# Row-tiled logits and indexer scores in layer 0 of a two-layer attention trunk (one Trainium2 core)

## Chip, cores and metric

One core of one Trainium2 chip runs the whole kernel in one launch. The metric is device time in microseconds, measured around the execution; lower is better. The engines named below: TensorE (PE in the profile, its weight loads PEld), VectorE (DVE), ScalarE (ACT), GpSimd (POOL) and SyncE (SP), which issues the DMAs.

## What is computed

The input x is 256 tokens by 1024 features, float32. Layer 0 is sparse attention with an indexer, layer 1 stick-breaking attention; each is gated, projected and added to the scaled input under a LayerNorm. What matters here is layer 0:

```python
q, k, v, g, qi, wi, ki = jnp.split(x @ w_in, cuts, axis=-1)   # 16 heads of 64; indexer: 8 heads of 64, one ki
q, k, qi, ki = (apply_rope(t) for t in (q, k, qi, ki))
rel = relu(einsum('bqhd,bsd->bqhs', qi, ki) * 64 ** -0.5)
score = einsum('bqhs,bqh->bqs', rel, wi)                      # keys in the same or an earlier chunk of 64
idx = top 64 keys of score, for each query
logits = einsum('bqhd,bqkhd->bhqk', q, k[idx]) * 64 ** -0.5
p = softmax(logits)
y = (einsum('bhqk,bqkhd->bqhd', p, v[idx]) * silu(g)) @ w_out
x = layer_norm(ALPHA * x + y)
```

## The kernel before

Matmul operands are kept in two float32r parts, a high part and the rest (names ending in h and l); a product is three matmuls (high x high, high x low, low x high). Weights come in 80 chunks of 512 KB. `fetch` (L73) issues a chunk's DMA on SyncE into one of four `raw` buffers, ScalarE copies its high part (`wh`, L63) and VectorE subtracts the rest (`wl`, L64); chunks are split two ahead of their use. A projection accumulates in a PSUM bank of the pool `pp` (three banks); transposes, scores, logits and values use the pool `at` (five banks).

Layer 0 begins with the indexer's projection (L208). Rope (`rope`, L191 to L198) is four VectorE steps, two products out of PSUM (L195 `ra`, L196 `rb`) and two sums (L197, L198). ki and qi are transposed to features by tokens and split. The split of ki is `pad_split` (L235): ki stands in both 64-row halves of the transposed tile, and each half is copied to its own 256 columns of a zeroed tile `zpad[0]`, by one ScalarE step (L229) and one VectorE step (L230) a half. With the other rows zero, one matmul over all 128 rows with 2n columns gives the scores of two heads, side by side in one bank.

`select` (L260) is a generator. For each token tile t (n = 128 or 256 keys) it has four steps, each with three such matmuls (`mm3`, L129 to L132), one relu on ScalarE (L270) and two additions on VectorE (L273), and then finds the 64 largest in eight rounds of a VectorE maximum (L279) and a replacement (L280), two rounds a step. `mix` (L119) steps it in turn with the first query, key and value blocks: 4 steps for each of the three blocks, 16 for `select`.

The main loop (L498) then runs eight head pairs through stages, one letter of "kfvFlft" each: k is `keys0` (two transposes of rotated keys, then `pad_split` into `zpad[j % 2]`), l is `logits0` one step later, t is `turn0` (transposes of the weights) two steps later, v is `values0` (`weighted_v`, L341, each head in its 64 columns of the array) three steps later; f takes a piece of the remaining projections, and F does so in the first four steps only. So in steps 4 to 8 the logits directly follow the values. `logits0` (L377) has three matmuls for each token tile through `mm3`; for each tile and head VectorE adds the mask and takes the extreme (L393), ScalarE takes the exponential (L398), VectorE scales (L400, L403).

The order of instructions on each engine's queue is laid down before the run by the framework: it goes by the program's order, and where an instruction isn't ready in its own estimate of times it puts later ones ahead. At run time every queue is worked off in that order. Layer 1 uses `zpad` again, for its queries.

Of the kernel before, what the change touches and what calls it, by code (L numbers as in the profile page):

```python
# [9 lines left out]
F32 = mybir.dt.float32  # L10
F32R = mybir.dt.float32r
AF = mybir.ActivationFunctionType
OP = mybir.AluOpType
# [29 lines left out]
def trunk(ctx: ExitStack, tc: tile.TileContext, x_rows, x_idx, w_all, consts, lnp, out):  # L43
# [13 lines left out]
    def as32(t):  # L57
        return t.bitcast(F32)
# [7 lines left out]
    # activations, feature-major: [feature in tile, tile, token], split in two float32r parts  # L66
# [29 lines left out]
    def load_block():  # L96
        """A quarter of [1024, 512] of a weight matrix after the other: two K tiles a chunk."""
        for _ in range(4):
            yield [w.rearrange("p (k n) -> p k n", k=2) for w in load_chunk()]

    def tok_part(outs, src, wc, c):
        """Adds a chunk's part to the token tiles in outs (tile, PSUM): the activations are stationary."""
# [7 lines left out]
    def tok_block(src):  # L110
        """Yields after every chunk but the last; returns the PSUM tiles."""
# [7 lines left out]
    def mix(*gens):  # L119
        """One step of every generator in turn."""  # L120
# [8 lines left out]
    def mm3(ps, sh, sl, mh, ml, first, last):  # L129
        nc.tensor.matmul(ps, sh, mh, start=first, stop=False)  # L130
        nc.tensor.matmul(ps, sh, ml, start=False, stop=False)
        nc.tensor.matmul(ps, sl, mh, start=False, stop=last)  # L132

    def proj_feat(ps, src, chunk):
        """[128 features, 256 tokens]: the weights are stationary."""
# [6 lines left out]
    # the tensor engine's clock comes up while the first loads are under way  # L142
# [6 lines left out]
    # ---------------------------------------------------------------- loads  # L149
# [33 lines left out]
    zpad = []  # L183
    for i in range(2):
        zh = cst.tile([P, 2, S], F32R, name=f"zh{i}")
        zl = cst.tile([P, 2, S], F32R, name=f"zl{i}")
        nc.gpsimd.memset(as32(zh), 0.0)
        nc.gpsimd.memset(as32(zl), 0.0)
        zpad.append((zh, zl))
# [10 lines left out]
    # ---------------------------------------------------------------- layer 0: indexer  # L200
# [39 lines left out]
    # indexer: qi of two heads stationary, ki moving, once for either head  # L240
    kz = zpad[0]
# [4 lines left out]
    pad_split(kz, pt[:, :S])  # L246
# [12 lines left out]

    def select():  # L260
        for t in range(NT):
            n = (t + 1) * P
            ts = slice(t * P, (t + 1) * P)
            sc = sb.tile([P, n], F32, name=f"sc{t}")
            prev = adm[t]
            for j in range(4):
# [415 lines left out]
```

## Time and profile before

| | us |
|---|---|
| three runs | 319.74, 318.9, 317.7 |
| median | 318.9 |
| span of the profiled execution, first to last instruction | 318.4 |
| what lies around the span (median less span) | 0.5 |
| TensorE busy | 304.0 |
| VectorE busy | 238.5 |
| ScalarE busy | 186.7 |

The profile is of one execution; its own time isn't listed apart from its span. Times in the views are from the span's start. A row of a timeline gives start, length, engine, line, operation, output and inputs, shapes, count, and in brackets the idle time before it and what ended it; consecutive instructions of one kind are one row, and a matmul's length reaches past the start of the next one, so its cost is read from start to start.

### The profile page before, as it was taken

How to read it: one execution, taken by the hardware profiler on the slowest of the kernel's cores; microseconds unless marked ns; L12 is line 12 of the kernel's file. 1: busy time of each engine (PE TensorE's matmuls, PEld its weight loads, DVE VectorE, ACT ScalarE, POOL GpSimd, SP SyncE). 2: the span in 40 equal slices, each digit the busy share in tenths (PEclk: the TensorE clock that was granted, in tenths of full speed). 3: DMA queues.
4: the chain of work that ended last, by engine and by line, in shares of the span. 5: the costliest groups of instructions: out<-in, count | busy, mean ns of one | idle time of the engine just before them, and what ended most of it. 6: DMA issues, size and time to landing. Idle time of an engine off the chain costs nothing.

```text
span 318.4 us, 5179 instructions
## 1 busy us (share of the span) xinstructions
PE 304.0 (95%) x1914; PEld 264.2 (83%) x1914; DVE 238.5 (75%) x514; ACT 186.7 (59%) x365; POOL 7.8 (2%) x16
## 2 busy tenths in 40 slices
PE   8997899996999999999999999999999999999990
PEld 5985788885887899987788889999999999987790
DVE  3777999997998899897389667655677767662475
ACT  5655545664336997876306276556698888965200
POOL 3010000000000000000010100000000000000011
PEclk9999999999899999999999999999999999999997
DMA  7799744784233745665422949866543433000003
GB/s 263 249 324 307 271 141 143 236 264 153 59 95 118 258 136 153 193 203 178 134 66 80 294 134 320 282 192 165 189 148 118 110 103 118 2 1 1 2 2 130
DMA packets 14425, 50.44 MB, mean 158 GB/s; under 512 B 1600, under 2 KB 1728, under 8 KB 14400
## 3 DMA queue, kind: packets, MB, share of 16 engines
q1 hardware_dynamic: 14256, 49.97, 48.9%
q8 instruction: 15, 0.25, 0.4%
q10 hardware_dynamic: 144, 0.14, 0.1%
q14 instruction: 10, 0.08, 0.1%
HBM read 49.05 MB, written 1.05 MB: 157 GB/s over the span
## 4 chain that ended last, share of the span: by engine, by line
PE 73%; DMA 11%; DVE 10%; ACT 3%; issue 2%; DVEq 0%; SPq 0%; ACTq 0%
PE bank L139 29%; PE bank L107 28%; DMA raw<-w_all 9%; DVE wl L64 4%; PE bank L347 3%; DMA raw<-x_idx 2%; ACT wh L63 2%; PE bank L348 1%; PE bank L571 1%; PE bank L130 1%; DVE sc L280 1%; PE bank L549 1%; PE bank L548 1%; PE bank L550 1%; PE bank L132 1%
## 5 line engine op out<-in xcount | busy, mean ns | idle before, releaser
L63 ACT ACTIVATE wh<-raw 128x1024 fp32r<-128x1024 f32 (+2 forms) x89 | 90.1, 1015 | 58.9 <-DMA raw<-w_all 25.7
L64 DVE TENSOR_TENSOR wl<-raw,wh 128x1024 fp32r<-128x1024 f32 (+2 forms) x89 | 103.5, 1164 | 28.1 <-ACT wh L63 27.2
L107 PE MATMUL bank<-wh,xTh 128*128 128x512 f32 x96 | 28.6, 411 | 2.6 <-DVE rb L196 2.5
L107 PE MATMUL bank<-wh,xTl 128*128 128x512 f32 x96 | 27.9, 400 | 0.0
L107 PE MATMUL bank<-wl,xTh 128*128 128x512 f32 x96 | 27.5, 395 | 0.0
L139 PE MATMUL bank<-yTh,wh 128*128 128x256 f32 x192 | 27.4, 285 | 0.0
L139 PE MATMUL bank<-yTl,wh 128*128 128x256 f32 x192 | 26.9, 283 | 0.0
L139 PE MATMUL bank<-yTh,wl 128*128 128x256 f32 x192 | 26.9, 283 | 0.0
L139 PEld LDWEIGHTS bank<-yTh,wh 128*128 128x128 f32 x192 | 24.7, 190 | 1.2 <-DVE sl L64 0.7
L139 PEld LDWEIGHTS bank<-yTh,wl 128*128 128x128 f32 x192 | 24.8, 192 | 0.0
L139 PEld LDWEIGHTS bank<-yTl,wh 128*128 128x128 f32 x192 | 24.7, 192 | 0.0
L107 PEld LDWEIGHTS bank<-wh,xTh 128*128 128x128 f32 x96 | 17.8, 194 | 7.3 <-issue 3.6
L107 PEld LDWEIGHTS bank<-wh,xTl 128*128 128x128 f32 x96 | 18.5, 194 | 3.9
L107 PEld LDWEIGHTS bank<-wl,xTh 128*128 128x128 f32 x96 | 18.0, 188 | 3.7
L107 PE MATMUL bank<-wh,oh 128*128 128x512 f32 (+1 forms) x80 | 20.8, 355 | 0.0
L107 PE MATMUL bank<-wh,ol 128*128 128x512 f32 (+1 forms) x80 | 20.5, 352 | 0.0
L107 PE MATMUL bank<-wl,oh 128*128 128x512 f32 (+1 forms) x80 | 20.4, 350 | 0.0
L557 DVE SCALAR_TENSOR_TENSOR ab<-bank,ab 128x512 f32<-128x512 f32 (+1 forms) x16 | 8.2, 553 | 12.8 <-ACT ab L556 12.8
L107 PEld LDWEIGHTS bank<-wl,oh 128*128 128x128 f32 x80 | 14.0, 188 | 2.2
L107 PEld LDWEIGHTS bank<-wh,ol 128*128 128x128 f32 x80 | 13.9, 188 | 2.3 <-issue 0.2
L107 PEld LDWEIGHTS bank<-wh,oh 128*128 128x128 f32 x80 | 13.6, 189 | 2.2 <-issue 0.3
L398 ACT ACTIVATE p<-ml,mx 128x128 f32<-128x128 f32 (+1 forms) x32 | 14.3, 447 | 1.1 <-DVE mx L393 0.6
(148 smaller groups left out, 552.3 us busy)
## 6 DMA issues: line engine op xcount, KB each, us to landing
raw<-w_all SPq DMA_DIRECT2D x80, 512.0 KB, 4.2
raw<-x_idx SPq DMA_DIRECT2D x7, 420.0 KB, 3.9
gb<-lnp SPq DMA_DIRECT2D x4, 512.0 KB, 7.0
x<-x_rows SPq DMA_DIRECT2D x2, 512.0 KB, 6.1
y<-x SPq DMA_DIRECT2D x4, 256.0 KB, 2.1
cs<-consts SPq DMA_DIRECT2D x1, 512.0 KB, 7.0
raw<-x_idx SPq DMA_DIRECT2D x1, 288.0 KB, 3.0
raw<-x_idx ACTq DMA_DIRECT2D x1, 132.0 KB, 3.2
```

What stands on the lines that cost most here:

```text
L63: nc.scalar.activation(h, src, AF.Copy)
L64: nc.vector.tensor_sub(lo, src, as32(h))
L107: nc.tensor.matmul(ps, src[kk][xp][:, t * P:(t + 1) * P], wc[wp][:, k, :], start=kk == 0 and xp + wp == 0, stop=kk == 7 and wp == 1)
L130: nc.tensor.matmul(ps, sh, mh, start=first, stop=False)
L132: nc.tensor.matmul(ps, sl, mh, start=False, stop=last)
L139: nc.tensor.matmul(ps, w[wp][:, k, :], src[k][xp], start=k + xp + wp == 0, stop=k == 7 and wp == 1)
L280: nc.vector.match_replace(out=sc, in_to_replace=m8, in_values=sc, imm_value=NEG_REP)
L347: nc.tensor.matmul(po[rs, :S], vt[0][:, hs], p0(i), start=True, stop=False)
L348: nc.tensor.matmul(po[rs, P:S], vt[1][:, hs], p1(i), start=False, stop=True)
L398: nc.scalar.activation(p[:, i, :], m[:, i, :], AF.Exp, bias=mx[:, c], scale=-1.0, accum_out=sm[:, c])
L548: nc.tensor.matmul(pv, kh[:, ks], z[0][:, :, qs], start=True, stop=False)
L557: nc.vector.scalar_tensor_tensor(a, pv, 0.0, a, op0=OP.max, op1=OP.add)
```

## The change

In layer 0 the zero padding goes. A new helper issues the three products of two heads alternately, each head on its own 64 rows of the array and into its own bank; a bank holds both token tiles (columns 0 to 128 and 128 to 384). The split of the keys of a head pair, and of ki, is one step on ScalarE and one on VectorE over 128 rows. `select` runs both token tiles in each of its four score steps, so it has 12 steps. The two relus of a step are one per head (128x384). The zeroed tiles are made after layer 0, in the same memory as the keys (tags zh0 to zl1). Comments and docstrings go.

```diff
-    def mm3(ps, sh, sl, mh, ml, first, last):
-        nc.tensor.matmul(ps, sh, mh, start=first, stop=False)
-        nc.tensor.matmul(ps, sh, ml, start=False, stop=False)
-        nc.tensor.matmul(ps, sl, mh, start=False, stop=last)
-
...
-    zpad = []
-    for i in range(2):
-        zh = cst.tile([P, 2, S], F32R, name=f"zh{i}")
-        zl = cst.tile([P, 2, S], F32R, name=f"zl{i}")
-        nc.gpsimd.memset(as32(zh), 0.0)
-        nc.gpsimd.memset(as32(zl), 0.0)
-        zpad.append((zh, zl))
+
+    def kpart(name, i):
+
+        return cst.tile([P, S], F32R, name=name, tag=f"z{name[-1]}{i}")
...
+    def rows_mm(ps, sh, sl, mh, ml):
+
+        for n, (a, b) in enumerate(((sh, mh), (sh, ml), (sl, mh))):
+            for i in range(2):
+                r = slice(i * HD, (i + 1) * HD)
+                nc.tensor.matmul(ps[i], a[r], b[r], start=n == 0, stop=n == 2)
...
-    pad_split(kz, pt[:, :S])
+    kih, kil = kpart("kih", 1), kpart("kil", 1)
+    feat_split(kih, kil, pt[:, :S])
...
+    cols = (slice(0, P), slice(P, 3 * P))
+
     def select():
...
+        scs, prev = [], list(adm)
+        for t in range(NT):
+            scs.append(sb.tile([P, (t + 1) * P], F32, name=f"sc{t}"))
+        for j in range(4):
+            pv = [bank(at, 3 * P) for _ in range(2)]
+            for t in range(NT):
+                n = (t + 1) * P
+                ts = slice(t * P, (t + 1) * P)
+                rows_mm([v[:, cols[t]] for v in pv], qih[:, j, ts], qil[:, j, ts], kih[:, :n], kil[:, :n])
+            rel = []
+            for a in range(2):
+                r = wk.tile([P, 3 * P], F32, name=f"rel{a}", tag="p256")
+                nc.scalar.activation(r, pv[a], AF.Relu, scale=SCALE)
+                rel.append(r)
+            for t in range(NT):
                 for a in range(2):
                     h = 2 * j + a
-                    nc.vector.scalar_tensor_tensor(sc, rel[:, a, :], wi[t][:, h:h + 1], prev,
+                    nc.vector.scalar_tensor_tensor(scs[t], rel[a][:, cols[t]], wi[t][:, h:h + 1], prev[t],
                                                    op0=OP.mult, op1=OP.add)
-                    prev = sc
-                yield
+                    prev[t] = scs[t]
+            yield
+        for t in range(NT):
+            n = (t + 1) * P
+            sc = scs[t]
...
     def keys0(j):
-        z = zpad[j % 2]
         pt = bank(at)
         for t in range(NT):
             nc.tensor.transpose(pt[:, t * P:(t + 1) * P], kr[t][:, 2 * j:2 * j + 2, :], ident)
-        pad_split(z, pt[:, :S])
+        kh, kl = kpart("kh", j % 2), kpart("kl", j % 2)
+        feat_split(kh, kl, pt[:, :S])
+        held["k", j] = kh, kl
 
     def logits0(j):
-        z = zpad[j % 2]
+        kh, kl = held.pop(("k", j))
+        pa = [bank(at, 3 * P) for _ in range(2)]
+        for t in range(NT):
+            n = (t + 1) * P
+            ts = slice(t * P, (t + 1) * P)
+            rows_mm([v[:, cols[t]] for v in pa], qh[j][:, ts], ql[j][:, ts], kh[:, :n], kl[:, :n])
...
-            pv = bank(at, 2 * n).rearrange("p (a s) -> p a s", a=2)
-            mm3(pv, qh[j][:, ts], ql[j][:, ts], z[0][:, :, :n], z[1][:, :, :n], True, True)
...
-                nc.vector.tensor_tensor_reduce(m[:, i, :], pv[:, i, :], negm[t], scale=1.0,
+                nc.vector.tensor_tensor_reduce(m[:, i, :], pa[i][:, cols[t]], negm[t], scale=1.0,
...
     load_gb(1)
...
+    zpad = []
+    for i in range(2):
+        zh = cst.tile([P, 2, S], F32R, name=f"zh{i}", tag=f"zh{i}")
+        zl = cst.tile([P, 2, S], F32R, name=f"zl{i}", tag=f"zl{i}")
+        nc.gpsimd.memset(as32(zh), 0.0)
+        nc.gpsimd.memset(as32(zl), 0.0)
+        zpad.append((zh, zl))
```

## Rows read from the trace of the kernel before

**Rows 1.** The page, busy time by engine: us (share of the span), instructions.
```profile
PE 304.0 (95%) x1914; PEld 264.2 (83%) x1914; DVE 238.5 (75%) x514; ACT 186.7 (59%) x365; POOL 7.8 (2%) x16
```

**Rows 2.** Stretches: PE, PEld, DVE, ACT, POOL busy (count), granted clock, DMA share, GB/s.
```profile
40.00:75.20 35.20, 35.20 (x162) 28.68 (x160) 33.44 (x78) 18.62 (x26) 0.00 (x0) 1.00 0.65 207
...
78.95:82.30 3.35, 3.35 (x9) 2.60 (x8) 3.35 (x12) 0.00 (x0) 0.00 (x0) 0.50 0.01 2
```

**Rows 3.** The chain that ended last, 58 to 84 us: start, length, what.
```profile
68.97 5.42 DMA raw<-w_all
...
76.92 0.70 DVE rb L196
```

**Rows 4.** Timelines of ACT, DVE and PE at the hole before 77.76 us.
```profile
71.63 0.38 ACT L229 ACTIVATE zh<-bank 64x256 fp32r<-64x256 f32 x1
...
73.01 0.67 DVE L195 TENSOR_TENSOR ra<-bank,cs 128x512 f32<-128x512 f32 x1
...
75.91 0.43 DVE L230 TENSOR_TENSOR zl<-bank,zh 64x256 fp32r<-64x256 f32 x1 [1.89 <-ACT zh L229]
...
77.76 0.70 PE L107 MATMUL bank<-wh,xTh 128*128 128x512 f32 x2 [2.48 <-DVE rb L196]
```

**Rows 5.** Timelines of ACT and PE at the first indexer scores.
```profile
31.21 0.36 ACT L229 ACTIVATE zh<-bank 64x256 fp32r<-64x256 f32 x1
32.39 0.38 ACT L229 ACTIVATE zh<-bank 64x256 fp32r<-64x256 f32 x1 [0.82 <-DVE zl L230]
...
32.87 0.59 PE L130 MATMUL bank<-zh,qih 128*128 128x256 f32 x3 [1.92 <-issue]
```

**Rows 6.** Timeline of PE, the logits of one head pair.
```profile
102.28 0.28 PE L130 MATMUL bank<-zh,qh 128*128 128x256 f32 x1
...
102.64 0.39 PE L130 MATMUL bank<-zh,qh 128*128 128x512 f32 x1
...
103.33 0.62 PE L107 MATMUL bank<-wh,xTh 128*128 128x512 f32 x2
```

**Rows 7.** Timeline of PE, values: one head alone (97.63), two together (109.91).
```profile
97.63 0.65 PE L347 MATMUL bank<-pT,vt 128*64 128x256 f32 x2
...
98.43 0.96 PE L107 MATMUL bank<-wh,xTh 128*128 128x512 f32 x3
...
109.91 0.66 PE L347 MATMUL bank<-pT,vt 128*64 128x256 f32 x4
```

**Rows 8.** Timeline of PE, the end of the values and the logits behind them.
```profile
110.51 0.27 PE L348 MATMUL bank<-pT,vt 128*64 128x128 f32 x1
110.71 0.39 PE L130 MATMUL bank<-zh,qh 128*128 128x256 f32 x1
110.94 0.28 PE L131 MATMUL bank<-zl,qh 128*128 128x256 f32 x1
```

**Rows 9.** Timeline of PE, transposes of 128 columns, each with a load of its own.
```profile
114.73 0.27 PE L412 MATMUL bank<-cs,p 128*128 128x128 f32 x1
114.84 0.27 PE L413 MATMUL bank<-cs,p 128*128 128x128 f32 x1
```

**Rows 10.** Timelines of DVE and PE: a weight split and its first use.
```profile
40.82 1.22 DVE L64 TENSOR_TENSOR wl<-raw,wh 128x1024 fp32r<-128x1024 f32 x1
...
43.92 1.07 PE L107 MATMUL bank<-wl,xTh 128*128 128x512 f32 x4
```

**Rows 11.** Groups of DVE by shape: count, busy us, mean ns, idle before.
```profile
L230 DVE TENSOR_TENSOR zl<-bank,zh 64x256 fp32r<-64x256 f32 x18 | 7.5, 419 | 3.7 <-ACT zh L229 3.5
...
L279 DVE MAX8 m<-sc 128x8 f32<-128x256 f32 x8 | 3.3, 417 | 0.0
...
L273 DVE SCALAR_TENSOR_TENSOR sc<-rel,wi,sc 128x256 f32<-128x256 f32 x7 | 3.3, 474 | 0.0
```

**Rows 12.** Timeline of DVE, the second tile's first score addition and what follows it.
```profile
55.88 0.47 DVE L273 SCALAR_TENSOR_TENSOR sc<-rel,wi,cs 128x256 f32<-128x256 f32 x1
56.26 0.08 DVE L280 MATCH_VALUE_LOAD sc<-m,sc 128x8 f32 x1
```

More of the change, by code (lines that the diff above doesn't have):

```diff
@@ L238, in pad_split @@
             feat_split(z[0][r, i, :], z[1][r, i, :], src[r, :], scale)
-    kz = zpad[0]
+    def rows_mm(ps, sh, sl, mh, ml):
[3 more added lines that the diff above has]
+                nc.tensor.matmul(ps[i], a[r], b[r], start=n == 0, stop=n == 2)
     pt = bank(at)
@@ L258, in trunk @@
     negm = []
+    cols = (slice(0, P), slice(P, 3 * P))
     def select():
+        scs, prev = [], list(adm)
[13 more added lines that the diff above has]
+            for t in range(NT):
+                for a in range(2):
+                    h = 2 * j + a
+                    nc.vector.scalar_tensor_tensor(scs[t], rel[a][:, cols[t]], wi[t][:, h:h + 1], prev[t],
+                                                   op0=OP.mult, op1=OP.add)
+                    prev[t] = scs[t]
+            yield
         for t in range(NT):
             n = (t + 1) * P
[L263 to L266, printed above, removed]
-                pv = bank(at, 2 * n).rearrange("p (a s) -> p a s", a=2)
-                mm3(pv, qih[:, j, ts], qil[:, j, ts], kz[0][:, :, :n], kz[1][:, :, :n], True, True)
-                rel = wk.tile([P, 2, S], F32, name="rel", tag="p256")[:, :, :n]
-                nc.scalar.activation(rel, pv, AF.Relu, scale=SCALE)
-                for a in range(2):
-                    h = 2 * j + a
-                    nc.vector.scalar_tensor_tensor(sc, rel[:, a, :], wi[t][:, h:h + 1], prev,
-                                                   op0=OP.mult, op1=OP.add)
-                    prev = sc
-                yield
+            sc = scs[t]
             for i in range(TOPK // 8):
@@ L384, in logits0 @@
             n = (t + 1) * P
-            ts = slice(t * P, (t + 1) * P)
-            pv = bank(at, 2 * n).rearrange("p (a s) -> p a s", a=2)
-            mm3(pv, qh[j][:, ts], ql[j][:, ts], z[0][:, :, :n], z[1][:, :, :n], True, True)
             m = wk.tile([P, 2, n], F32, name=f"ml{t}", tag=f"b{n}")
```

## The prediction

> **What bounds the kernel now.** I read the page first (busy shares), then busy time by stretches with the granted clock, then the chain that ended last in order of time, then the timelines of ScalarE, VectorE and TensorE around the two places where TensorE stood still, then the matmuls of the changed stage one by one. TensorE is busy for 95% of the span [rows 1]; from 40 to 75.2 us it has no idle time at all, with VectorE busy for 33.4 of those 35.2 us [rows 2]. So the reader is to see a TensorE-bound kernel with VectorE close behind in layer 0, and two holes. The large one ends at 77.76 us: 2.48 us idle until VectorE's rope step (rb, L196) frees a PSUM bank [rows 4]. The chain tells why that is late: a weight chunk issued at 68.97 lands 5.42 us later [rows 3], ScalarE's split of it runs, then the second half of the key split of head pair 1 on ScalarE (zh, L229), its other part on VectorE at 75.91 (zl), and only then rb at 76.92 [rows 3, 4]. The first half of that key split had run on ScalarE at 71.63; VectorE had begun the rope with ra at 73.01 and then stood for 1.89 us [rows 4]. Right behind that hole the granted clock is 0.50 from 78.95 to 82.30, the 1.2 GHz level, where it was 1.00, 2.4 GHz, before [rows 2]: with TensorE busy throughout, 3.35 us do the work of 1.7, so 1.7 are lost. The second hole ends at 32.87: 1.92 us idle before the first indexer scores, which need the second half of the indexer's key split (ScalarE 32.39 to 32.77; the first half had run at 31.21) [rows 5].
>
> **Part 1, the matmuls of a head pair.** Now six per pair: three of 256 and three of 512 columns, 102.28 to 103.33, 1.05 us, or 0.12 and 0.23 each [rows 6]; half of what is multiplied is zero padding. After: twelve of 64 rows, two at a time, three pairs of 128 and three of 256 columns. Do pairs run side by side? No row shows two row halves, but the value matmuls use column halves: one head alone takes 97.63 to 98.43, 0.80 us, and two heads together 109.91 to 110.71, 0.80 us [rows 7, 8]. I take full overlap. A pair of 256 columns then costs 0.12 [rows 6]. A pair of 128 columns lies between 0.06 (half of that) and the time of its weight loads: where a load of this type stands bare it adds 0.11 (0.39 against 0.28 us) [rows 8], and 128-column transposes, each with its own load, start every 0.11 [rows 9]. I take 0.11, the nearer row. Sum: 3 x 0.11 + 3 x 0.12 = 0.68, that is 0.37 less per pair; from below 0.53.
>
> The loads double in number and none is shorter for having half the rows. The Trainium skill (TensorE: Matmul & The Clock Gate, "LDWEIGHTS (loading the stationary operand)") says that a load goes by its columns and not its rows; the bare 0.11 agrees with its 107 ns for 128. The same page, in Part 3, has loads overlap running matmuls only where the row groups differ; by that a group would be 3 x (0.11 + 0.06) + 3 x (0.11 + 0.12) = 1.2 us, but the 256-column matmuls with a new load each start every 0.12 [rows 6], so for the whole array the trace doesn't bear it out.
>
> **Part 2, changes of tiling.** Going from column halves back to the whole array costs: the last matmul starts at 110.51, the next load at 110.71, where 0.11 would have done [rows 8, 9], and that load stands bare for another 0.11: 0.20 us in all. No row shows a change into row halves; bounds 0 and 0.20, I take 0.20, each way. (The Trainium skill, TensorEngine Tiling (Array Packing), "Key Properties", has every change of mode drain the engine.) In the loop "kfvFlft" the logits of pairs 3 to 7 come straight after the values, so they pay an entry already: 0.68 + 0.20 against 1.05, a gain of 0.17 each. Pairs 0 to 2 and the four score steps of the indexer pay both ways: 0.68 + 0.40 against 1.05, a loss of 0.03 each. Sum 0.2 - 0.85 = -0.6 us. The matmul saving is thus mostly spent on switching.
>
> **Part 3, the key split in one piece.** Nine times one ScalarE op and one VectorE op (419 ns) go [rows 11]; beside a full TensorE that is worth nothing by itself. But both holes hang on the second halves. At 75: with one op at 71.63, VectorE has no wait after ra (73.68), runs rb by 74.7, and the bank is free before TensorE asks (77.76 less 2.48, so 75.3): -2.5 us, and with it the idle time that the clock's fall followed: -1.7. Bound: 0, if another wait stands there. What is late next: the weight splits have run ahead by then, so nothing near. At 31: the scores can start at 31.6 instead of 32.87, up to -1.2.
>
> **Part 4, scores of both token tiles in one step.** The step now yields four times instead of twice four, so the eight score additions of the second tile, at 56 us and after now, move up to the query stage. Each holds VectorE for 0.4 (474 ns long, but the next instruction starts 0.38 behind it) [rows 11, 12]: 3.2 us. There they stand ahead of the weight split at 40.82, as the first tile's do now; it ends at 42.04 and TensorE needs it at 43.92 [rows 10], 1.9 us to spare, or 0.7 if TensorE comes 1.2 earlier. The key split saves 0.4 there, so the split is 2.8 us late and TensorE waits 2.1: instead of 1.2 ahead it is 0.9 behind. Bounds: -1.2 (the scheduler puts the split first) and +3.2. The top 64 of the second tile (16 ops of 0.41 us) [rows 11] also move up, from behind these additions to beside the value stage; I take no wait from them, bound 3.3 (half of them ahead of a split). The two relus of a step (128x384, where 128x256 and 128x512 stood) are the same columns. They take both buffers of tag p256, so the next step's relu waits for this step's additions; ScalarE's splits run ahead there, taken as 0.
>
> **Part 5, the rest.** Four GpSimd memsets move to the end of layer 0, over tiles that the last logits free; layer 1 first needs them after its value projection and its gates, tens of us on. GpSimd has only the norm's powers queued: 0. Both heads' tiles of a pair now lie in one bank each, so the mask step of the first tile waits for the second tile's matmuls, some 0.3 us; the transposes that need it come a whole step later: 0.
>
> Sum on the profiled execution: +0.9 - 2.5 - 1.7 - 0.6 = -3.9, from its span of 318.4 to 314.5. The median of the three runs (318.9) lies 0.5 above that span, which I take for what lies around it: 315.0.
>
> **Rivals.**
> B, the wait at 75 stays: the new order puts the single key split behind the chunk that lands at 74.4, or other VectorE work takes its place. For: both sit in in-order queues whose order is planned anew. Against: the transposes for it were done in time for a split at 71.63. Then +0.9 - 0.6: 319.2.
> C, the weight loads of the two halves go one after the other (or don't hide under the matmuls): twelve loads of 0.11 are 1.32 us for a group, above its 1.05 of now; 0.64 more than in my sum, twelve groups, +7.7: 322.7. It decides as soon as a group takes over 0.9 us. For: no row has a half-row load. Against: two 64-column halves with a load each end in the time of one [rows 7, 8]. By the rule of the page above it would be 0.52 more a group, 321.2.
> D, VectorE becomes the bound from 36 to 60 us: additions and half the top 64 ahead of the splits (3.2 + 3.3, less the 0.4 saved and the 1.9 to spare: 4.2 late), the score steps broken up between projection matmuls, one more change both ways in each (1.6), and the wait at 75 only changes its shape: +4.2 + 1.6 - 0.6, 324.1. It decides once the splits make TensorE over 4 us late, which the vanished hole no longer pays. For: VectorE is full there. Against: splits have 1.9 us and more to spare.
> E, better: 128-column pairs at 0.06 (-1.8) and the gain at 31 us kept, with no wait at 44 (-2.1): 311.1.
>
> **Chances.** My forecast A 0.50, B 0.17, C 0.13, D 0.13, E 0.07. About 1% is what a measurement tells here: 315.7 and 322.1 are the bounds. A, from 312.5 to 317.5, gives 0.36 faster, 0.11 same, 0.03 slower; B 0.02, 0.09, 0.06; C 0, 0.03, 0.10; D 0, 0.04, 0.09; E 0.07 faster. Together 0.45, 0.27, 0.28. The range 311.5 to 322.5 leaves out some of D, part of C and the best of E; A's own is 312.5 to 317.5.
>
> **What would show it.** Right: no TensorE idle of over 1 us between 70 and 85 us and a clock of 1.00 there; a logits group near 0.7 us, its two halves starting within some hundredths; a gap of about 0.2 at each change of tiling; a wait of about 2 us near 42 to 46. Wrong: halves that start one after the other (C); a bare wait on rope or on a split after 60 us with a clock of 0.50 behind it (B, D); score matmuls strewn singly among the projections (D). The forecast as a whole falls if the hole at 75 remains.

## The result and the profile after

Four runs of the kernel after have a median of 322.25 us (320.94 to 324.97), four of the kernel before 318.3 us (316.42 to 319.74). The measured ratio is 1.0145, 95% interval 1.0097 to 1.0192 (the two medians alone give 1.0124): the change makes the kernel slower by 1 to 2%. The forecast said 315.0.

The two profiles alone would not have told this. The execution that the profile of after shows is the fastest of its four (320.94 us, span 319.2), so 1.74 us lie around a span, and 1.73 to 1.86 in every later run. By that the profiled execution of before (span 318.4) took about 320.1 us. The experiments brought 59 more executions of the kernel before: median 317.75 us, with a mean granted clock of 0.990 to 0.997 in 48 of them (median 317.4) and 0.987 to 0.989 in 11 (median 319.5). The profiled one, with 0.988 and some 320.1 us, is like the 11; only 3 of the 59 took over 320. After had 0.978 to 0.987 in all four. The mean doesn't tell where a fall of the clock lay: every trace has a stretch at 0.50 behind TensorE's last matmul, and in one version a trace with a mean of 0.992 has another in its middle. One later run, of the version with padded scores and row-half logits (321.83 us, mean clock 0.977), was slow and is left out of that version's ratio.

The page of after, busy time by engine, answers to [rows 1]: TensorE has 1.3 us less work and the span is longer.

```profile
PE 302.7 (95%) x1986; PEld 262.0 (82%) x1986; DVE 236.4 (74%) x505; ACT 182.6 (57%) x356; POOL 7.9 (2%) x16
```

The timeline of TensorE at the logits of one head pair (answers to [rows 6] and [rows 8]: the values, the logits behind them, and the projection that follows):

```profile
111.92 0.40 PE L357 MATMUL bank<-pT,vt 128*64 128x128 f32 x4
112.25 0.33 PE L237 MATMUL bank<-kh,qh 64*128 64x128 f32 x2
112.41 0.28 PE L237 MATMUL bank<-kl,qh 64*128 64x128 f32 x2
112.53 0.27 PE L237 MATMUL bank<-kh,ql 64*128 64x128 f32 x2
112.64 0.33 PE L237 MATMUL bank<-kh,qh 64*128 64x256 f32 x2
112.80 0.28 PE L237 MATMUL bank<-kl,qh 64*128 64x256 f32 x2
112.92 0.28 PE L237 MATMUL bank<-kh,ql 64*128 64x256 f32 x2
113.13 0.74 PE L134 MATMUL bank<-xTh,wh 128*128 128x256 f32 x4
```

Each row is two matmuls, one in each half of the rows, that run side by side: the next row starts 0.11 to 0.12 us later, as behind one matmul of that width, and 0.16 behind the first row of either width. From the first logits to the next projection it is 112.25 to 113.13, 0.88 us, where the padded group took 1.05 [rows 6]. What a pair saves is read from one pair's logits to the next pair's, since the bare load behind a change of tiling stood in the padded group and now stands in the projection behind the logits (timelines of TensorE, before and after):

```profile
119.38 0.39 PE L130 MATMUL bank<-zh,qh 128*128 128x256 f32 x1
```

```profile
120.75 0.33 PE L237 MATMUL bank<-kh,qh 64*128 64x128 f32 x2
```

It is 8.67 us before (110.71 [rows 8] to 119.38) and 8.50 after (112.25 to 120.75), 0.17 less. That is Part 1 and Part 2 as forecast.

Where TensorE stands still (its timeline, the rows with idle time over 0.2 us between 30 and 100 us):

```profile
30.14 0.78 PE L237 MATMUL bank<-kih,qih 64*128 64x128 f32 x4 [0.27 <-ACT kih L221]
...
40.86 0.70 PE L107 MATMUL bank<-wh,xTh 128*128 128x512 f32 x2 [2.99 <-DVE rb L188]
...
79.97 0.70 PE L107 MATMUL bank<-wh,xTh 128*128 128x512 f32 x2 [2.08 <-DVE rb L188]
...
95.52 0.66 PE L314 MATMUL bank<-cs,rq 128*128 128x128 f32 x4 [0.74 <-DVE rq L190]
```

The 1.92 us before the first indexer scores [rows 5] have shrunk to 0.27. The 2.48 us before 77.76 [rows 4] are still there, as 2.08 before 79.97. Two waits are new: 2.99 us before 40.86 and 0.74 before 95.52. The first one hurts twice, as the stretches of after show (busy time and count of PE, PEld, DVE, ACT, POOL, then granted clock, DMA share, GB/s):

```profile
36.00:41.50 5.50, 2.51 (x12) 1.79 (x11) 5.50 (x13) 4.10 (x6) 0.00 (x0) 1.00 0.94 323
41.50:44.90 3.40, 3.40 (x19) 2.57 (x17) 3.40 (x7) 1.06 (x1) 0.00 (x0) 0.50 0.20 47
77.00:82.30 5.30, 3.22 (x21) 2.09 (x20) 5.30 (x17) 1.06 (x1) 0.00 (x0) 1.00 0.59 216
```

Behind the wait of 2.99 us the clock is granted at 0.50, the 1.2 GHz level, for 3.4 us, that is 1.7 us lost. In this execution it stays at 1.00 behind the wait of 2.08. In the profile of before the fall came behind the wait at 77 [rows 2].

Both long waits are for `rb` (L188), the rope step that frees the PSUM bank which the next block's second token tile needs (`pp` has three). What VectorE does ahead of it, first in the kernel before (timeline of VectorE):

```profile
35.23 0.69 DVE L195 TENSOR_TENSOR ra<-bank,cs 128x512 f32<-128x512 f32 x1
35.84 0.68 DVE L196 TENSOR_TENSOR rb<-bank,cs 128x512 f32<-128x512 f32 x1
36.44 0.34 DVE L273 SCALAR_TENSOR_TENSOR sc<-rel,wi,cs 128x128 f32<-128x128 f32 x1
```

And in the kernel after (timeline of VectorE):

```profile
30.79 3.49 DVE L64 TENSOR_TENSOR wl<-raw,wh 128x1024 fp32r<-128x1024 f32 x3
34.19 0.74 DVE L279 SCALAR_TENSOR_TENSOR sc<-rel,wi,cs 128x128 f32<-128x128 f32 x2
34.85 2.21 DVE L279 SCALAR_TENSOR_TENSOR sc<-rel,wi,sc 128x128 f32<-128x128 f32 x6
36.98 1.22 DVE L64 TENSOR_TENSOR wl<-raw,wh 128x1024 fp32r<-128x1024 f32 x1
38.11 1.40 DVE L279 SCALAR_TENSOR_TENSOR sc<-rel,wi,sc 128x128 f32<-128x128 f32 x4
39.43 0.68 DVE L187 TENSOR_TENSOR ra<-bank,cs 128x512 f32<-128x512 f32 x1
40.03 0.68 DVE L188 TENSOR_TENSOR rb<-bank,cs 128x512 f32<-128x512 f32 x1
```

The reader is to see the order. Before, the first score addition stands behind `rb`, and between the key split and `ra` there are two weight splits. After, twelve additions (34.19 to 36.98 and 38.11 to 39.43, 4.1 us) and four weight splits stand ahead of `ra`. VectorE has no idle time in these rows; it works off its queue, and `rb` starts at 40.03 instead of 35.84. TensorE has been at the bank since 37.87 (40.86 less 2.99).

At 80 us it is the same engine with other work (timeline of VectorE of after):

```profile
72.96 1.22 DVE L64 TENSOR_TENSOR wl<-raw,wh 128x1024 fp32r<-128x1024 f32 x1 [1.66 <-ACT wh L63]
...
77.50 0.41 DVE L222 TENSOR_TENSOR kl<-bank,kh 128x256 fp32r<-128x256 f32 x1
77.83 0.41 DVE L288 MAX8 m<-sc 128x8 f32<-128x256 f32 x1
78.16 0.67 DVE L187 TENSOR_TENSOR ra<-bank,cs 128x512 f32<-128x512 f32 x1
...
79.14 0.68 DVE L188 TENSOR_TENSOR rb<-bank,cs 128x512 f32<-128x512 f32 x1
```

The key split is one piece now (`kl`, 77.50), yet the rope is as late as ever: VectorE stood 1.66 us for a weight chunk's high part, and two more splits, the key split and rounds of the second tile's top 64 come before the rope.

### The profile page after: what moved, and what is told of

It is laid out like the page before. It is cut to its first block, busy times and chain, and to the rows that moved or that the text cites. A ratio compares the mean times of both kernels' runs of the same rounds, so it can differ in the third digit from the quotient of the medians.

```text
span 319.2 us, 5327 instructions
## 1 busy us (share of the span) xinstructions
PE 302.7 (95%) x1986; PEld 262.0 (82%) x1986; DVE 236.4 (74%) x505; ACT 182.6 (57%) x356; POOL 7.9 (2%) x16
## 3 DMA queue, kind: packets, MB, share of 16 engines
HBM read 49.05 MB, written 1.05 MB: 157 GB/s over the span
## 4 chain that ended last, share of the span: by engine, by line
PE 82%; DMA 7%; DVE 7%; issue 2%; ACT 2%; SPq 0%; DVEq 0%; ACTq 0%
PE bank L107 37%; PE bank L134 29%; DMA raw<-w_all 4%; DMA raw<-x_idx 3%; PE bank L356 3%; PE bank L237 2%; DVE wl L64 2%; PE bank L590 1%; PE bank L357 1%; DVE rb L188 1%; ACT wh L63 1%; PE bank L568 1%; PE bank L567 1%; PE bank L569 1%; DVE ra L187 1%
## 5 line engine op out<-in xcount | busy, mean ns | idle before, releaser
L107 PEld LDWEIGHTS bank<-wh,xTh 128*128 128x128 f32 x96 | 17.0, 188 | 9.4 <-issue 5.8
L63 ACT ACTIVATE oh<-og 128x256 fp32r<-128x256 f32 x16 | 6.7, 418 | 15.8 <-DVE og L335 15.8
```

Source lines behind the costliest of these rows:

```text
L63: nc.scalar.activation(h, src, AF.Copy)
L107: nc.tensor.matmul(ps, src[kk][xp][:, t * P:(t + 1) * P], wc[wp][:, k, :], start=kk == 0 and xp + wp == 0, stop=kk == 7 and wp == 1)
```

## The experiments

All twelve compute the whole reference; none leaves work out. Three stretches tell where a version wins or loses: from TensorE's first transposes of the indexer (`ri`, about 25 us) to its first transposes of the second query block (`rq`, about 92 us), from there to the end, and, in the middle, TensorE's wait for `rb` in the first query block. In brackets behind the first stretch: how long TensorE is idle in it, and how many stretches of 3.4 us at half clock it has. All but the medians and ratios is from one trace of each version; times in us. A ratio is to runs of before made alongside, so it isn't a quotient of the medians shown:

| kernel | median, ratio to before [95%] | additions ahead of that `rb` | `rb` starts | wait for it | 25 to 92 (idle; at half clock) | 92 to end |
|---|---|---|---|---|---|---|
| before | 317.75 (59 runs) | 0 | 35.84 | under 0.15 | 67.6 (4.4; 1) | 225.5 |
| after | 322.25, 1.0145 [1.0097, 1.0192] | 12 | 40.03 | 2.99 | 68.2 (5.4; 1) | 225.7 |
| tiles in turn | 319.91, 1.0084 [1.0059, 1.0110] | 4 | 37.22 | 1.83 | 67.0 (2.9; 0) | 225.0 |
| merged, padded | 316.25, 0.9972 [0.9940, 1.0004] | 5 | 37.65 | under 0.15 | 64.0 (1.8; 0) | 225.5 |
| merged, padded, again | 316.82, 0.9962 [0.9930, 0.9994] | 5 | 38.18 | under 0.15 | 64.8 (2.9; 0) | 225.6 |
| four turns later | 324.70, 1.0219 [1.0169, 1.0270] | 0 | 35.67 | 1.00 | 72.6 (6.9; 2) | 225.0 |
| logits only | 318.01, 0.9998 [0.9967, 1.0030] | 0 | 35.45 | under 0.15 | 64.1 (1.8; 0) | 224.6 |
| padded, bank per head | 320.91, 1.0116 [1.0064, 1.0168] | 12 | 39.61 | 2.13 | 67.2 (3.3; 1) | 226.2 |
| two turns later | 321.53, 1.0122 [1.0083, 1.0161] | 4 | 38.09 | 0.49 | 68.3 (4.6; 1) | 225.2 |
| padded scores, row logits | 318.18, 1.0004 [0.9968, 1.0039] | 5 | 37.99 | under 0.15 | 63.9 (2.4; 0) | 226.1 |
| ReLU per tile | 322.73, 1.0146 [1.0075, 1.0217] | 11 | 40.24 | 2.80 | 69.8 (6.5; 1) | 225.6 |
| in turn, three later | 323.06, 1.0134 [1.0070, 1.0197] | 0 | 34.95 | 0.91 | 70.1 (5.0; 1) | 224.8 |
| merged, padded, narrow | 322.26, 1.0135 [1.0079, 1.0192] | 12 | 42.50 | 1.33 | 69.3 (5.6; 0) | 226.4 |
| every other turn | 320.59, 1.0116 [1.0054, 1.0178] | 4 | 35.79 | 0.50 | 67.7 (5.0; 0) | 225.1 |

The last column hardly moves (224.6 to 226.4); the second last runs from 63.9 to 72.6. The loss is made between 25 and 92 us. The trace of before is of one of its longer executions; and up to five projection matmuls of 0.23 us change sides at 92 from version to version, so differences under 1 us between two rows say little.

One thing goes with the loss in every row. When VectorE comes to `rb` of the first key block (48 to 56 us), it has done 19 weight splits in before and in the four rows whose ratio is about 1 or below, and 22 or 23 in the nine that are slower. A split holds VectorE for some 1.1 us. So it is not the additions alone that the new orders put ahead of the ropes; no run here moves the splits by themselves.

**Row halves alone, token tiles in turn.** The kernel after, with `select` going through the token tiles one after the other as before.

```diff
-        for j in range(4):
-            pv = [bank(at, 3 * P) for _ in range(2)]
-            for t in range(NT):
...
+        for t in range(NT):
...
+            for j in range(4):
+                pv = [bank(at, n) for _ in range(2)]
+                rows_mm(pv, qih[:, j, ts], qil[:, j, ts], kih[:, :n], kil[:, :n])
```

> The changed kernel with the indexer's token tiles scored one after the other again, as before the change; all matmuls stay in row halves, key splits in one piece. Theory Q (the second tile's score additions stand ahead of the query block's rope on VectorE, and TensorE waits for the PSUM bank that the rope frees): the 2.99 us hole at 40.9 us shrinks below 1.5 us, no half clock behind it, and the time falls from 322.25 to 318 to 320. Theory R (row halves and changes of tiling cost TensorE more than they save): nothing changes in the matmuls, so 321.5 to 323.

Measured 319.91 us: some 2 us of the loss are gone, 2.6 stay. In the traced execution (318.78 us) no fall of the clock is left between 10 and 300 us, but a wait of 1.83 us for the query rope, where I expected under 1.5 (timeline of TensorE of this version):

```profile
38.05 0.70 PE L107 MATMUL bank<-wh,xTh 128*128 128x512 f32 x2 [1.83 <-DVE rb L188]
```

VectorE has four splits and four additions ahead of `rb` here; so the merging of the tiles is a part of the loss and not all of it. Nor is what stays a matter of waits: TensorE is idle for 2.9 us between 25 and 92, as in the second trace of the merged, padded version below, which loses nothing. It is busy for 64.0 us there against 61.9, and it goes into row halves and back eight times where after does so four times. So here the row halves with their changes of tiling seem to cost TensorE more than they save; that is the rival theory's mechanism, though not its 321.5 to 323.

**The merging alone, padded.** The kernel before, with both token tiles in each score step; wide padded matmuls, one bank and one ReLU per tile.

```diff
-        for t in range(NT):
...
-            for j in range(4):
+        for j in range(4):
+            rel = []
+            for t in range(NT):
                 pv = bank(at, 2 * n).rearrange("p (a s) -> p a s", a=2)
                 mm3(pv, qih[:, j, ts], qil[:, j, ts], kz[0][:, :, :n], kz[1][:, :, :n], True, True)
```

> The kernel before with one edit: each score step of the indexer takes both token tiles; matmuls keep all 128 rows and the zero padding. Theory Q: a hole of 2 us or more near 40 us, before the query rope, that the kernel before doesn't have, and 320.5 to 323. Theory R: within 1 us of the kernel before (318.3).

Measured 316.25 us, no slower than before; neither range held it. My theory of that moment, that moving the additions up is by itself what costs, fell. A second set of runs was to narrow the interval:

> The kernel before with both token tiles in each score step and padded matmuls, a second time, for a narrower interval. If its 0.9972 [0.994, 1.0004] is a gain, the ratio comes out again between 0.994 and 0.999; if it was chance, at 0.999 to 1.003. By the order on VectorE (two additions ahead of ra more than before, with each followed by other work) I expect no difference or a gain under 0.5%.

It came out at 0.9962 [0.9930, 0.9994]: a gain of some 0.4%, small, but the only version here that beats both kernels. Its timeline of VectorE shows why nothing waits:

```profile
36.15 0.34 DVE L277 SCALAR_TENSOR_TENSOR sc<-rel,wi,sc 128x128 f32<-128x128 f32 x1
36.41 0.47 DVE L277 SCALAR_TENSOR_TENSOR sc<-rel,wi,cs 128x256 f32<-128x256 f32 x1
36.92 0.69 DVE L195 TENSOR_TENSOR ra<-bank,cs 128x512 f32<-128x512 f32 x1
37.53 0.74 DVE L277 SCALAR_TENSOR_TENSOR sc<-rel,wi,sc 128x256 f32<-128x256 f32 x2
38.18 0.68 DVE L196 TENSOR_TENSOR rb<-bank,cs 128x512 f32<-128x512 f32 x1
```

Its `rb` starts 2.3 us later than before's and 1.85 earlier than after's. TensorE comes to the bank 1.1 us later than in after, mainly since it has stood for 1.98 us at the first scores (0.27 in after), and takes it up at 39.01 without a wait (timeline of TensorE):

```profile
38.75 0.39 PE L107 MATMUL bank<-wh,xTl 128*128 128x512 f32 x1
...
39.01 0.70 PE L107 MATMUL bank<-wh,xTh 128*128 128x512 f32 x2
```

So the 1.65 us that after gains at the first scores are no gain in time: it only comes to the rope earlier.

**The scores four turns later.** The kernel after with four empty turns (a turn is one step of `mix`) ahead of the score steps; another version has two.

```diff
     def select():
+        for _ in range(4):
+            yield
         scs, prev = [], list(adm)
         for t in range(NT):
```

> The changed kernel with four empty steps ahead of the indexer's scoring, so that it begins beside the key block and stands behind the query block's rope. Theory Q: no hole over 1 us near 40 us, 317 to 320. Theory R: 321.5 to 323. The hole near 80 us may stay or move in either case.

> The changed kernel with two empty steps ahead of the scoring, so that four additions instead of twelve stand ahead of the query rope and none right ahead of the key rope. Theory S: no hole over 1.2 us near 40 or 56 us, 316.5 to 319.5. Theory T: as the changed kernel, 321 to 323.

Measured 324.70 and 321.53 us. Both miss what I expected: the wait at the query rope falls to 1.00 and 0.49, and the additions now stand ahead of the next rope, that of the first key block. With four turns TensorE also waits 1.20 us for a weight split before 34.08, and the clock falls twice in this stretch (timeline of TensorE):

```profile
56.06 0.70 PE L107 MATMUL bank<-wh,xTh 128*128 128x512 f32 x2 [3.15 <-DVE rb L188]
```

With two turns:

```profile
56.38 1.19 PE L107 MATMUL bank<-wh,xTh 128*128 128x512 f32 x2 [2.24 <-DVE rb L188]
```

So moving the scores in the program doesn't take the wait away; it moves to the rope that a long run of VectorE work now stands ahead of.

**The logits only.** The kernel before with the row halves in the main loop alone (`keys0`, `logits0`, the key split in one piece); the indexer is padded as before.

```diff
     def keys0(j):
...
-        pad_split(z, pt[:, :S])
+        kh, kl = kpart("kh", j % 2), kpart("kl", j % 2)
+        feat_split(kh, kl, pt[:, :S])
...
     def logits0(j):
+            rows_mm([v[:, cols[t]] for v in pa], qh[j][:, ts], ql[j][:, ts], kh[:, :n], kl[:, :n])
...
-            mm3(pv, qh[j][:, ts], ql[j][:, ts], z[0][:, :, :n], z[1][:, :, :n], True, True)
```

> The kernel before with only the main loop's part of the change: keys split in one piece, logits in row halves; the indexer as before with its zero padding. Theory Q: no hole near 40 us, 316.5 to 318.5 (the matmuls give 0.17 us for each of five head pairs, the hole near 77 us may stay). Theory R: 320 to 323.

Measured 318.01 us, no difference that the interval shows; it leaves room for a gain of up to 0.3%, about what was expected. The shorter groups are there, but TensorE comes earlier to the transposes of the second query block (in before four projection matmuls and three transposes of weights lie between its first two and the other six; here they come behind) and waits for its rope (timeline of TensorE of this version):

```profile
91.85 0.65 PE L319 MATMUL bank<-cs,rq 128*128 128x128 f32 x4 [0.76 <-DVE rq L203]
```

All versions with row halves in the main loop show a wait for `rq` here, 0.59 to 0.85 us; those that are padded throughout don't. It takes back nearly all of the 0.85 us that Part 2 has for pairs 3 to 7. The traced execution (316.18 us) is the fastest of its ten; what the others spend their 1.8 us more on isn't traced.

This version has before's order on VectorE around 75 us, with the key split of the head pair in one piece (timeline of VectorE, then of TensorE):

```profile
72.70 0.40 DVE L235 TENSOR_TENSOR kl<-bank,kh 128x256 fp32r<-128x256 f32 x1
...
74.35 0.67 DVE L201 TENSOR_TENSOR rb<-bank,cs 128x512 f32<-128x512 f32 x1
```

```profile
75.16 0.71 PE L107 MATMUL bank<-wh,xTh 128*128 128x512 f32 x2 [0.59 <-DVE rb L201]
```

Nothing makes the rope wait here, and `rb` starts at 74.35, close to the 74.7 of Part 3.

**The form of the step, padded.** The kernel before with the step of after (a bank and one ReLU of 384 columns per head), but with padded matmuls on the whole array; the main loop is before's.

```diff
+        for j in range(4):
+            pv = [bank(at, 3 * P) for _ in range(2)]
...
+                for a in range(2):
+                    mm3(pv[a][:, cols[t]], qih[:, j, ts], qil[:, j, ts], kz[0][:, a, :n], kz[1][:, a, :n], True, True)
```

> The kernel before with the score step in the form of the change (both token tiles in a step, a bank and one relu for each head over 384 columns, four additions), but every matmul over all 128 rows with the zero padding, and the main loop as before. Theory S (that form makes a step's four additions ready at once, so that twelve of them are laid ahead of the query rope on VectorE): a hole of 2 us or more near 40 us, 319.5 to 322.5. Theory T (the row halves and the one-piece key split bring the scores too early): no hole over 1 us near 40 us, 317 to 319, the padded matmuls costing some 0.3 us more in each of four steps.

Measured 320.91 us, 1.0116 [1.0064, 1.0168]: most of the loss without a single row half. An estimated 1.3 of its 3.7 us is the time of the narrower padded matmuls themselves, as I expected (0.33 a step, worked out below at the merged, padded, narrow version). The wait is there, and so is the clock's fall behind it (timeline of TensorE, then the stretch behind it):

```profile
40.44 1.14 PE L107 MATMUL bank<-wh,xTh 128*128 128x512 f32 x2 [2.13 <-DVE rb L196]
```

```profile
40.50:43.90 3.40, 3.40 (x11) 2.72 (x11) 3.40 (x8) 1.06 (x1) 0.00 (x0) 0.50 0.08 29
```

**Merged padded scores and row-half logits.** The scores of the merged, padded version with the main loop of the logits-only version.

> Scores of both tiles in a step with padded matmuls and a relu for each tile (as the second experiment), and the main loop of the change (keys in one piece, logits in row halves). If the row halves give what the matmuls show, 0.17 us for each of five pairs, without disturbing the order: 314.5 to 316.5. If what the fourth experiment lost comes from the main loop itself: 316.5 to 318.5.

Measured 318.18 us, 1.0004 [0.9968, 1.0039]: again no gain from the row-half logits. Its timeline of TensorE has the two waits behind one another, the first with a key split in one piece; the merged, padded version, whose key split is in two halves, waits 0.34 us there:

```profile
76.06 0.70 PE L107 MATMUL bank<-wh,xTh 128*128 128x512 f32 x2 [1.18 <-DVE rb L201]
...
91.50 0.77 PE L324 MATMUL bank<-cs,rq 128*128 128x128 f32 x5 [0.74 <-DVE rq L203]
```

So a key split in two halves doesn't bring the wait at 75, nor does one in one piece take it away. Here a weight split at 72.77, for which VectorE waits 0.36 us on ScalarE, stands between the key split and the rope.

**A ReLU per tile.** The kernel after, with four ReLUs of 128 or 256 columns in a step.

```diff
-            for a in range(2):
-                r = wk.tile([P, 3 * P], F32, name=f"rel{a}", tag="p256")
-                nc.scalar.activation(r, pv[a], AF.Relu, scale=SCALE)
+            for t in range(NT):
+                n = (t + 1) * P
+                r = wk.tile([P, 2, S], F32, name=f"rel{t}", tag="p256")[:, :, :n]
+                for a in range(2):
+                    nc.scalar.activation(r[:, a, :], pv[a][:, cols[t]], AF.Relu, scale=SCALE)
```

> The kernel after, with a ReLU per token tile and head (four to a step, of 128 or 256 columns) in place of one of 384 columns per head; banks, row halves and matmuls as after. If the form of the step delays the query rope (the additions of a step become ready together, and VectorE's order lays them ahead of ra and rb), then with 9 in place of 12 additions laid ahead of ra TensorE's hole at about 40.9 us shrinks from 2.99 to 1.2 to 2.4 us, by three additions of about 0.3 us each and the earlier start of the first, and the time is 319.0 to 321.5 us. If the bank per head is what delays, and the ReLUs have no part in it, the hole stays at 2.7 us or more and the time at 321.5 to 323.5 us.

Measured 322.73 us and a wait of 2.80: the second of the two outcomes in its numbers, so the ReLU's form has no part in the loss. That the bank per head has a part, as that outcome had it, doesn't follow; the narrow version below loses without one. Nine additions stand ahead of `ra`, but two more and a fifth split are put in before `rb`, which starts at 40.24, no earlier than in after.

**The tiles in turn, three turns later.** Row halves, tiles in turn, three empty turns, so that both ropes of the query block stand ahead of every addition.

> The row halves with the token tiles in turn, and the score steps three steps later, so that VectorE's order has both ropes of the query block ahead of all additions. If only the rope's place in VectorE's order costs, the hole at about 38 us (1.84 us in the version with the tiles in turn) is gone, no fall of the clock is left, and the time is 315.5 to 318.5 us, at or below the kernel before. If the additions that are moved back come to stand before the key rope instead, as in the version two steps later, a hole of 1.5 us or more opens between 50 and 60 us, and the time is 319 to 322 us.

Measured 323.06 us: the second of the two outcomes in kind, and worse than its 319 to 322. The query rope waits 0.91 us, and the key rope 3.11 (timeline of TensorE):

```profile
54.80 0.70 PE L107 MATMUL bank<-wh,xTh 128*128 128x512 f32 x2 [3.11 <-DVE rb L188]
```

**Merged, padded, narrow.** The merged, padded version with six matmuls of n columns in place of three of 2n. Bank per tile, ReLU per tile, no row halves.

```diff
-                mm3(pv, qih[:, j, ts], qil[:, j, ts], kz[0][:, :, :n], kz[1][:, :, :n], True, True)
+                for a in range(2):
+                    mm3(pv[:, a, :], qih[:, j, ts], qil[:, j, ts], kz[0][:, a, :n], kz[1][:, a, :n], True, True)
```

> The version with both token tiles in each padded score step (the one that came out at 0.996 of before), with one edit: the three matmuls of 2n columns of a tile are six of n columns, one head each, into the same bank. Banks, ReLUs (one per tile) and the 16 additions stay, and no row halves are used. The order laid down for VectorE then has all 12 additions of three steps ahead of the first ra, where the version with wide matmuls has 3. If that order is what costs, and neither the row halves nor the bank per head, TensorE shows a hole of 2 to 3 us before the second token tile of the first key block at about 40 us, and the time is 319.5 to 322.5 us. If a bank or a ReLU per head is needed for the loss, the hole stays under 0.5 us and the time is 315.5 to 317.5 us.

Measured 322.26 us, 1.0135 [1.0079, 1.0192], as slow as after, though the matmuls compute the same columns. Twelve additions stand ahead of the rope, as expected, and five weight splits where the wide version has three; `rb` starts at 42.50, 4.3 us later than in the wide version (timeline of VectorE, the last four of the additions and the rope):

```profile
40.46 1.40 DVE L278 SCALAR_TENSOR_TENSOR sc<-rel,wi,sc 128x128 f32<-128x128 f32 x4
...
42.50 0.68 DVE L196 TENSOR_TENSOR rb<-bank,cs 128x512 f32<-128x512 f32 x1
```

The wait is smaller than expected, because TensorE comes later too (timeline of TensorE):

```profile
43.32 0.70 PE L107 MATMUL bank<-wh,xTh 128*128 128x512 f32 x2 [1.33 <-DVE rb L196]
```

The profiled spans of the two differ by 5.3 us. An estimated 1.3 of it are the narrow matmuls themselves: a step of 6 x 0.11 and 6 x 0.12 ([rows 9], [rows 6]) against 1.05, four times. The waits between 40 and 60 us add 2.2 (1.33, 0.37 and 0.69 against 0.24), the one before 81 us another 0.7 (1.34 against 0.64). The other 1.1 us isn't accounted for. So neither row halves nor banks nor ReLUs by head are needed for the loss. An order on VectorE that puts the scores first, eleven or twelve additions with four or five splits ahead of `rb`, is in all four versions that merge the tiles, don't move the scores back and are slower than before (after, padded with a bank per head, ReLU per tile, narrow).

**Every other turn.** The kernel after with an empty turn ahead of each score step.

```diff
         for j in range(4):
+            yield
             pv = [bank(at, 3 * P) for _ in range(2)]
```

> The kernel after with a score step only in every second turn (an empty one ahead of each), so that four additions stand ahead of the query rope and eight ahead of the first key rope, with no round of the top 64 before it. If VectorE's order before the two ropes is what costs, the hole at about 40 us is under 0.7 us, the one at about 55 us under 1.2 us (2.24 us in the version two steps later, which had 12 additions and two rounds there), and the time is 317 to 319.5 us. If VectorE's work between 30 and 60 us is simply too much, whatever its order, the two holes together stay above 2.5 us and the time at 320.5 to 323 us.

Measured 320.59 us (319.34 in the profiled execution). The two waits came out as expected, 0.50 and 1.01 us; the time did not. Further waits came instead, 0.86 us for the rope before 40.19, 0.68 before 77.96, and (timeline of TensorE) one for the value block's bank, which ScalarE frees:

```profile
64.67 0.50 PE L107 MATMUL bank<-wh,xTh 128*128 128x512 f32 x1 [1.47 <-ACT vt L343]
```

## Why the prediction was wrong

**Part 1 was right in the main.** The two halves run side by side: a pair starts 0.11 us (128 columns) or 0.12 us (256) behind the one before, 0.16 us behind the first of either width. Rival C is out.

**Part 2 was right in its matmuls and not in its effect.** A padded group behind the values took 1.05 us and the 0.11 of a bare load; the new one takes 0.88 from its first matmul to the next projection's, with the change out of row halves in it (112.92 to 113.13, 0.21), and the bare load now falls to that projection. I had 0.17 less per pair, and that is what the rows give (8.67 to 8.50). But the step that called this a gain in time failed: the pairs of the main loop run between projection blocks whose ropes VectorE has to do, and nearly all that TensorE saves it waits, 0.74 us before 95.52 of after and 0.76 in the logits-only version. The ratio of that version is 0.9998, of the one with padded, merged scores 1.0004; both intervals leave room for a gain of 0.3%, and neither shows one.

**Part 3 failed, in two ways.** The step that failed is "What is late next: the weight splits have run ahead by then, so nothing near". In the profile of before the large hole did hang on the second half [rows 4], and in the logits-only version, with before's order and the split in one piece, the rope comes as forecast. But after has another order on VectorE: three weight splits, the first behind 1.66 us of waiting for a late chunk, and the top-64 rounds stand ahead of the rope, and the wait is 2.08 us. In the merged, padded version the key split is in two halves and the wait is 0.34 and 0.64. The rope waits for all that is queued ahead of it on VectorE, and any split that waits for a late chunk will do. This is rival B's outcome. The step that took the hole and the fall of the clock from one execution, 4.2 us in all, over-priced it as well: that execution, at some 320.1 us, is 2.4 us above the median of 59, and a mean clock of 0.989 or less came in 11 of them. How long the usual execution of before waits there isn't traced. The logits-only version, whose indexer and first blocks are before's own, shows 64.1 us from 25 to 92 where the profile of before has 67.6; the longer wait (2.48 against 0.59) and the fall (1.7) are as much as that difference. The merged, padded version waits 0.34 and 0.64 us there in its two profiles, with no fall. The small hole at 31 us did go, as forecast (1.92 to 0.27), and brought no time: TensorE stood at the rope instead.

**Part 4 had the mechanism, at the wrong place and too small.** The additions do stand ahead of something TensorE needs, but not of the weight split that I looked at ([rows 10]). They stand ahead of the rope, which frees a PSUM bank. I had 2.1 us of wait; it is 2.99, and a fall of the clock behind it, 1.7. The step that failed is "there they stand ahead of the weight split at 40.82, as the first tile's do now". In program order a turn now adds four additions where it added two, with three turns ahead of the rope; I moved the second tile's eight behind the first tile's places and did not ask how the whole order would come out: two more weight splits came ahead of the rope as well. This was rival D's direction (VectorE sets the end from 36 us on), which I had given 0.13.

**The base was wrong by 1.2 us.** What lies around the span is 1.75, not 0.5: the median of the runs was no measure of the profiled execution.

**Put together**, the forecast's -3.9 us falls apart as follows for the median: Part 3's -4.2 and the 0.6 of Part 2 did not come, and Part 4's +0.9 came out at about +4. That is what is left over of the loss, not a measurement; in the trace of after it is 2.99 and 1.7 less the 1.65 gained at the first scores, 3.0. That 322.25 lies inside the range 311.5 to 322.5 is luck: the range reached so far up for rivals C and D, of which C didn't come and D came in its direction only. By its own sign the forecast falls, since the hole at 75 remains. The padded version with a bank per head shows most of that loss (1.0116 against 1.0145), the version with the tiles in turn 2.6 us of it (1.0084), but each of the two has a part of its own in it, the narrow padded matmuls in the one and TensorE's longer work in the other.

**What stays open.** That the long run of VectorE work ahead of a rope makes TensorE wait is shown. How much of it the score additions make and how much the three or more weight splits that come ahead of the first key rope with them is not. Why the framework lays the additions ahead of the rope when the scores are computed by narrow matmuls, and behind it when by wide ones, was not looked into; banks, ReLUs and row halves are ruled out as conditions. Nor was a version found that keeps row halves in the scores and has the ropes early without clogging the next one: three attempts (two, three and four turns later) moved the wait to the key rope, a fourth (every other turn) spread it over four places. Whether VectorE's total work between 25 and 92 us leaves row halves any gain at all is therefore not settled; no run here shows one.

## What to carry to other kernels

Where TensorE is busy for 95% and VectorE for all but a few per cent of the same stretch, price a matmul saving by what VectorE can follow: take the next instruction that frees a bank, and list everything that the change puts ahead of it on its in-order queue. When work is merged into fewer steps, look at the ropes, evictions and other bank-freeing steps first and at the weight splits second; moving the merged work along only chooses which of them waits. Never price a hole or a fall of the clock from one profile: compare that execution's own time with the spread of the runs first.

## What the runs showed of the hardware

- How long TensorE has waited doesn't tell by itself whether its clock falls. A stretch of 3.4 us at 0.50 came behind the waits of 2.48 us in before, 2.99 in after, 2.13 in the padded version with a bank per head, 2.24 two turns later, 3.11 in turn and three later, 3.15 four turns later, and in this last version also behind the 1.00 us before 36.5 (another wait of 1.20 us had ended 2.4 us earlier). None came behind 1.83 us with the tiles in turn, 1.98 in the merged, padded version, 2.08 in after, nor behind 2.80 us in the version with a ReLU per tile, where it followed the 1.71 us before 79.21 instead. The stretches of that version behind its two waits:

```profile
41.10:44.50 3.40, 3.40 (x23) 2.50 (x23) 3.40 (x7) 1.29 (x2) 0.00 (x0) 1.00 0.65 246
80.60:83.90 3.30, 3.30 (x12) 2.42 (x12) 3.18 (x15) 2.07 (x6) 0.00 (x0) 0.50 0.00 1
```

- The change out of row halves takes 0.21 us from the last matmul's start to the next one's (112.92 to 113.13), as the change out of column halves did (0.20, [rows 8]).
- Three padded matmuls of 2n columns and six of n columns compute the same, but the six are slower: at 128 columns a matmul with its own load takes 0.11 us [rows 9], nearly as long as one of 256 (0.12, [rows 6]). I had used this for the row halves and not for what it makes of a padded step.
